# Layer trunk on one Trainium2 core: output projection of the mixer with unsplit fp32 weights, and PSUM banks as one region in the planned order

## The chip, the cores and the metric

The kernel runs on 1 core of a Trainium2 chip. The metric is device time in microseconds. Before the change it is 1097.59 us, the median of 3 runs (1096.93 to 1097.9).

## The reference

Input x is 256 tokens by 1024 features in fp32. Two layers follow each other; each adds half of a SwiGLU feed-forward, a mixer of two head groups, and half of a second feed-forward. A last RMSNorm gives the output. What matters here, from the reference:

```python
for l in range(DEPTH):                                   # DEPTH = 2
    x = x + 0.5 * swiglu(rms_norm(x, ffn1_norm[l]), ...) # 1024 -> 2816 -> 1024
    h = rms_norm(x, mix_norm[l])
    proj = h @ w_in[l]
    y_rwkv = rwkv7_group(proj[..., :RWKV_IN], ...)       # 512 features, a recurrence over chunks of 64
    y_ret = retnet_group(proj[..., RWKV_IN:])            # 512 features, retention in chunks of 64
    mixed = jnp.concatenate([y_rwkv, y_ret], axis=-1)
    x = x + mixed @ w_out[l]                             # 1024 x 1024
    x = x + 0.5 * swiglu(rms_norm(x, ffn2_norm[l]), ...)
return rms_norm(x, final_norm)
```

## The kernel before, in words

The 256 tokens are two tiles of 128 (t = 0 and 1), and each tile is a stream through the seven stages. `run` lets the two streams take turns, tile 1 two steps behind tile 0, so that both use a piece of weights soon after one another.

All weights lie in HBM as pieces of 128 x 2048 fp32, loaded in halves of 128 x 1024 (512 KB) through SyncE's queue into a ring of three raw buffers (`half`, line 616). ScalarE then rounds a half to fp32r (hi), VectorE subtracts it from the raw half (lo), and hi and lo go into two `wide` buffers of 4 KB per partition. Activations are split in the same way (`split`, line 645). A product of fp32 accuracy is then three fp32r matmuls, ah x wh, ah x wl and al x wh (`mm3`, line 639). A half stays in its two wide buffers until the later tile has used it.

The kernel isn't run in the order in which it is written. Every call is recorded as a node of a plan (`record`, line 231) with a price (`price`, line 291) and with its dependencies (`touch`, line 269, compares partitions and columns of a buffer). `simulate` (line 364) then plays the nodes on five engines, with 43 slots of 2 KB, 22 wide buffers and 8 PSUM banks, and gives each node a start. `schedule` (line 492) does this for several priorities (`GUIDES`, `SERIES`) and keeps the one whose modelled end is earliest. `emit` (line 512) issues all nodes in the order of their modelled starts; the tile framework under it then puts the semaphores, and does so by the order of emission. What `behind` and `in_turn` add are edges of the plan alone.

The steps around the change: `norm_T` (line 680) transposes a tile's x by TensorE, four blocks of 128x128 into one bank twice, and ScalarE and VectorE read each block into `parts` (hi and lo). `shifted` (line 766) and `ret_core` (line 1217) also fill a bank by several products and read it block by block. `rms`, `rwkv_key`, `ret_core` and `chain_out` raise a few numbers to -1/2 on GpSimd (`pow`, with operands named base in the trace). `inverse` (line 975) sends blocks through DRAM by SyncE's queue (d, mx, misc).

In the mixer (`mix`, line 1266) a string says the order of the steps of a tile: projections m, k, r, q, e, g, v, the retention R, the merge J, the chain a, b, c, and then W and w, the two halves of the output projection (retention heads and RWKV heads). W uses the pair rh, rl that `ret_out` (line 1252) makes; w uses mh, ml of `chain_end` (line 1163). Per tile and layer, W and w are 16 products of a 128x128 block with 512 columns, each three matmuls. Both tiles use the same wide buffers, so a half of w_out is loaded and split once per layer.

Of the kernel before, what the change touches and what calls it, by code (L numbers as in the profile page):

```python
# [12 lines left out]
F32 = mybir.dt.float32  # L13
F32R = mybir.dt.float32r
BF16 = mybir.dt.bfloat16
AF = mybir.ActivationFunctionType
ALU = mybir.AluOpType
# [5 lines left out]
P = 128  # L23
# [5 lines left out]
RW = 512  # L29
HD = 64  # L30
NRAW = 3
XG = (0, 8, 16)
XCUT = (2, 1)
WARM = 1
# [33 lines left out]
    return ap.unsqueeze(2).to_broadcast(shape)  # L68


PLACES = {"slot": (43, 2048), "wide": (22, 4096), "bank": (8, 2048)}
GUIDES = (5, 7, 10, 14, 20, 30)
SERIES = 3
TURN = -1.0
ENGINES = {"tensor": 0, "vector": 1, "scalar": 2, "gpsimd": 3, "sync": 4}

# [106 lines left out]
class Plan:  # L183
# [84 lines left out]

    def touch(self, op, v, write):
        b = v.buf  # L270
        m = v.bits()
        if not b.users or b.users[-1] is not op.node:
            b.users.append(op.node)
        for o, lo, hi, om in b.writes:
            if lo < v.hi and v.lo < hi and om & m:
                self.wait(op, o)
        if b.space == "bank" and op.node.eng == 0 and getattr(b, "tail", None) is not None:
            self.wait(op, b.tail)
        if write:
            for o, lo, hi, om in b.reads:  # L280
                if lo < v.hi and v.lo < hi and om & m:
                    self.wait(op, o)
            for l in (b.writes, b.reads):
                l[:] = [e for e in l if e[0].node is op.node or not (v.lo <= e[1] and e[2] <= v.hi and not e[3] & ~m)]
            b.writes.append((op, v.lo, v.hi, m))
            if b.space == "bank" and op.node.eng == 0:
                b.tail = op
        else:
            b.reads.append((op, v.lo, v.hi, m))

    def price(self, op):
        out, call, eng = op.args[0], op.call, op.eng
        if call == "dma_start":
            v = next(v for v in (op.outs + op.ins))
            n = (v.hi - v.lo) * v.cols[0].size * 4 if v.cols is not None else 65536
            op.cost, op.late, op.n = 60.0, 0.0, n
            op.form = "dma"
            return
        n = int(np.prod(out.shape[1:]))
        small = n < 32  # L300
        op.form = None
        if eng == "tensor":
            l = op.args[1] if call == "transpose" else op.kw["lhsT"]
            rows, cols = l.shape[0], int(np.prod(l.shape[1:]))
            if call == "matmul" and op.kw["rhs"].dt in (F32R, BF16):
                op.cost = 227.0 if n == 512 else 120.0
                op.late = (398 + n) / 2.4
                op.form = (128, 128)
            else:
                rows = 128 if rows > 64 else 64 if rows > 32 else 32  # L310
                cols = 128 if cols > 64 else 64 if cols > 32 else 32
                op.form = (rows, cols)
                op.cost = {(128, 128): 110.0, (64, 128): 55.0, (128, 64): 30.0, (64, 64): 29.0}.get(op.form, 13.0)
                if call == "matmul":
                    op.cost *= 2
                if n == 512:
                    op.cost = 860.0
                op.late = (398 + 2 * n) / 2.4
            op.late += 60
            return  # L320
        srcs = [v for v in op.ins]
        psum = any(v.buf.space == "bank" for v in srcs)
        col = any(v is not op.args[1] and isinstance(v, View) and int(np.prod(v.shape[1:])) == 1 and n > 8 for v in srcs)
        if eng == "scalar":
            op.cost = (193 + 0.742 * n if psum else 198 + 0.833 * n) + (75 if col else 0)
            f = op.args[2]
            op.form = {AF.Silu: "s", AF.Exp: "t"}.get(f)
        elif eng == "vector":
            if call == "tensor_tensor_scan":
                op.cost = 1224.0  # L330
            elif call in ("tensor_scalar", "tensor_copy", "memset") and not psum:
                op.cost = 150 + 0.52 * n
            elif call == "tensor_reduce":
                op.cost = 151 + 1.04 * int(np.prod(op.args[1].shape[1:]))
            elif len(out.shape) > 3 and out.shape[0] == 64:
                op.cost = 150 + 1.77 * n
            else:
                op.cost = 151 + 1.04 * n + (63 if col else 0)
        else:
            op.cost = 1100.0 if call == "memset" else 1000.0  # L340
        op.cost += 20
        op.late = op.cost + 55

# [20 lines left out]
    def simulate(self, prio):  # L364
# [14 lines left out]
        fabric = 0.0  # L379
        self.low = low = {}  # L380
        done, end, t = 0, 0.0, 0.0
# [7 lines left out]
        while done < total:  # L389
# [3 lines left out]
            t = heapq.heappop(events)  # L393
# [5 lines left out]
            for e in range(5):  # L399
# [49 lines left out]
                if form == "dma":  # L449
                    size = n.ops[0].n  # L450
                    begin = max(t, fabric)
                    fabric = begin + size / 330.0
                    land = fabric + (1700.0 if size > 70000 else 2100.0)
                    shift = land - t
                done += 1
                fin = t + dur
# [93 lines left out]
class Trunk:  # L550
    def __init__(self, plan, x, w, vecs, lora, fgain, consts, out):
# [13 lines left out]
        nc.scalar.dma_start(self.c[:, C_ID:C_ID + P], consts[:, C_ID:C_ID + P])  # L565
        self.load_x(0)
        self.raw = base[:, NBASE + 2 * D:].rearrange("p (n i) -> p n i", n=NRAW)
        self.nraw = 0
        self.consts_d = consts
        self.scan = self.c[:, C_SCAN:C_SCAN + 256].bitcast(BF16)  # L570
        nc.vector.memset(self.scan, 1.0)
# [44 lines left out]
    def half(self, i, h):  # L616

        if (i, h) not in self.wq:
# [7 lines left out]
            kind = sum(i % PIECES >= b for b in (33, 33 + FIRST, 46, 50)) % 4  # L626
            hi = self.A.get([P, 1024], "whi", F32R, kind)
            lo = self.A.get([P, 1024], "wlo", F32R, kind)
            nc.scalar.activation(hi, raw, AF.Copy)
            nc.vector.tensor_tensor(lo, raw, hi.bitcast(F32), op=ALU.subtract)  # L630
            self.wq[i, h] = (hi, lo)
        return self.wq[i, h]

    def weights(self, i, col, width):
        h, c = divmod(col, 1024)
        hi, lo = self.half(i, h)
        return hi[:, c:c + width], lo[:, c:c + width]

    def mm3(self, ps, ah, al, wh, wl, start, stop):
        nc = self.nc  # L640
# [522 lines left out]
    def chain_end(self, t, yf, rv):  # L1163
# [8 lines left out]
            nc.tensor.transpose(tr[:, p, :], yn[:, 2 * p:2 * p + 2].rearrange("q h d -> q (h d)"), self.ident)  # L1172
        TT(g, tr, g, op=ALU.mult)
        TT(g, g, bo, op=ALU.add)
        mh = A.get(full, "mh", F32R)
        ml = A.get(full, "ml", F32R)
        self.split(mh, ml, g)
        self.mixw[t] = (mh, ml)

    def ret_qk(self, t, ps):  # L1180
        nc, A = self.nc, self.A
# [70 lines left out]
    def ret_out(self, t, o_ps, rr, sq):  # L1252
# [5 lines left out]
        tr = self.A.bank(full, F32, name="tr")  # L1258
        for j in range(RH):
            nc.tensor.transpose(tr[:, j, :], sq[:, j, :], self.ident)  # L1260
        mh = A.get(full, "rh", F32R)
        ml = A.get(full, "rl", F32R)
        self.split(mh, ml, tr)
        self.mixr[t] = (mh, ml)

    def mix(self, t, base):
        nc, A = self.nc, self.A
        if t == 0:
# [3 lines left out]
            for i in range(2):  # L1272
# [6 lines left out]
            nc.vector.tensor_tensor(self.rkb, self.c[:, C_ONES:C_ONES + P].unsqueeze(1).to_broadcast([P, 4, P]),  # L1279
                                    self.vb(V_RK), op=ALU.mult)  # L1280
        self.norm_T(t, V_MIX)
        for step in PLAN[t]:
            if step in PROJ:
                blk, then = PROJ[step]
# [14 lines left out]
                self.ret_core(t)  # L1299
            else:  # L1300
                half = "Ww".index(step)
                mh, ml = (self.mixr, self.mixw)[half][t]
                for n in range(2):
                    ps = self.A.bank([P, 512], F32, name="gu")
                    for k in range(4):
                        wh, wl = self.weights(base + 13 + 2 * half + n, 512 * k, 512)
                        self.mm3(ps, mh[:, k, :], ml[:, k, :], wh, wl, k == 0, k == 3)
                        if k == 1:
                            yield
                    s = slice(512 * n, 512 * n + 512)  # L1310
# [157 lines left out]
```

## Time and profile before

| | |
|---|---|
| median of 3 runs | 1097.59 us |
| profiled execution, its own time | 1101.27 us |
| its span from first to last instruction | 1099.4 us |
| mean granted TensorE clock | 0.993 of full speed |
| busy: TensorE, weight loads, VectorE, ScalarE, GpSimd | 1062.5, 853.3, 661.4, 599.1, 38.1 us |
| moved by DMA | 181.57 MB, 165 GB/s in the mean |

How to read it: PE is TensorE's matmuls, PEld its weight loads, which overlap with them, DVE VectorE, ACT ScalarE, POOL GpSimd, SP SyncE. Matmuls are pipelined: each lasts longer than the time until the next can start, so busy time holds more than work. The trace names an instruction by tiles, out<-in: gu and acc are PSUM banks of projections and of the down projections, tr of transpositions and small products, wide the split weights, parts the split activations, base a large buffer that holds constants, x, the small columns and the raw ring. All records bear line 544, that of the emission, so tiles tell them apart. Every stop of an engine is put down to the semaphore that came last.

### The profile page before, as it was taken

To read this page: it belongs to the slowest core of one execution; us is meant where nothing else is said; L and a number is where in the kernel's file an instruction comes from. 1 tells how busy PE (TensorE), PEld (TensorE's weight loads), DVE (VectorE), ACT (ScalarE), POOL (GpSimd) and SP (SyncE) were. 2 spreads that over 40 slices of the span, in tenths; PEclk is the share of its full clock that TensorE was granted. 3 is DMA by queue.
4 is the path that set the end of the run, shared out by engine and by line. 5 is a ranking of instruction groups with operands and counts; after the bars stand their busy time and mean duration, and the time that the engine had idled before them with its cause. 6 is when DMAs were issued, how large, how long until landed. Compare 5 with 4: busy or idle time off the path is not lost.

```text
span 1099.4 us, 16122 instructions
## 1 busy us (share of the span) xinstructions
PE 1062.5 (97%) x6253; PEld 853.3 (78%) x6253; DVE 661.4 (60%) x1051; ACT 599.1 (54%) x1012; POOL 38.1 (3%) x44
## 2 busy tenths in 40 slices
PE   7999999899999999999999999999999999999997
PEld 5778888687877788778768887888877778877885
DVE  5656545577868755445555654546887786656532
ACT  6554444585768645444454554447767856454431
POOL 0000000011010000000000000000100100000000
PEclk9999999999999999999999999999999999999999
DMA  6656557443324466546545564665263236655541
GB/s 227 227 191 198 188 178 223 163 148 98 101 81 137 153 194 195 187 144 218 175 154 191 179 192 146 205 218 166 83 200 98 69 116 206 205 198 184 180 153 39
DMA packets 63772, 181.57 MB, mean 165 GB/s; under 512 B 18512, under 2 KB 18896, under 8 KB 63696
## 3 DMA queue, kind: packets, MB, share of 16 engines
q1 hardware_dynamic: 63264, 180.42, 50.8%
q8 instruction: 49, 0.80, 0.3%
q14 instruction: 27, 0.22, 0.1%
q10 hardware_dynamic: 432, 0.13, 0.1%
HBM read 178.17 MB, written 2.36 MB: 164 GB/s over the span
## 4 chain that ended last, share of the span: by engine, by line
PE 66%; DMA 15%; DVE 7%; ACT 5%; issue 5%; POOL 1%; ACTq 0%; POOLq 0%; DVEq 0%; SPq 0%
PE gu L544 39%; PE acc L544 19%; DMA base<-in_w 14%; PE tr L544 5%; DVE wide L544 4%; ACT wide L544 4%; PE ch L544 2%; PE pre L544 1%; POOL base L544 1%; ACT parts L544 1%; DMA base<-in_vecs 1%; DMA mx<-d 1%; DVE parts L544 0%; DMA d<-el 0%; ACT junk L544 0%
## 5 line engine op out<-in xcount | busy, mean ns | idle before, releaser
L544 PE MATMUL gu<-wide,parts 128*128 128x512 f32 (+1 forms) x2784 | 702.7, 396 | 8.0 <-ACT wide L544 2.8
L544 PEld LDWEIGHTS gu<-wide,parts 128*128 128x128 f32 x2784 | 508.6, 189 | 119.4 <-ACT wide L544 4.0
L544 ACT ACTIVATE wide<-base 128x1024 fp32r<-128x1024 f32 x332 | 349.9, 1059 | 333.9 <-DMA base<-in_w 214.3
L544 DVE TENSOR_TENSOR wide<-base,wide 128x1024 fp32r<-128x1024 f32 x332 | 401.2, 1221 | 203.2 <-ACT wide L544 145.7
L544 PE MATMUL acc<-wide,ht 128*128 128x512 f32 x1056 | 279.8, 396 | 0.7 <-ACT wide L544 0.6
L544 PEld LDWEIGHTS acc<-wide,ht 128*128 128x128 f32 x1056 | 196.9, 189 | 44.5 <-DVE wide L544 2.2
L544 DVE TENSOR_TENSOR ht<-tr,ht 128x256 fp32r<-128x256 f32 x88 | 37.0, 420 | 90.6 <-ACT ht L544 90.5
L544 POOL TENSOR_TENSOR base<-base 128x1 f32<-128x1 f32 (+2 forms) x26 | 33.2, 1277 | 977.3 <-DVE base L544 977.3
L544 DVE SCALAR_TENSOR_TENSOR hh<-gu,base,hh 128x256 f32<-128x256 f32 x88 | 42.1, 480 | 25.1 <-ACT hh L544 24.9
L544 ACT ACTIVATE hh<-gu,base 128x256 f32<-128x256 f32 x88 | 40.7, 464 | 28.3 <-PE gu L544 28.1
L544 DVE SCALAR_TENSOR_TENSOR parts<-tr,base,parts 128x128 fp32r<-128x128 f32 x96 | 30.6, 347 | 31.2 <-ACT parts L544 20.1
L544 ACT ACTIVATE parts<-tr,base 128x128 fp32r<-128x128 f32 x96 | 31.8, 365 | 31.7 <-PE tr L544 22.0
L544 PE MATMUL tr<-base,hh 128*128 128x128 f32 x176 | 43.3, 272 | 0.3 <-DVE ht L544 0.3
L544 ACT ACTIVATE ht<-tr 128x256 fp32r<-128x256 f32 x88 | 32.6, 371 | 15.7 <-PE tr L544 15.6
L544 PEld LDWEIGHTS tr<-base,hh 128*128 128x128 f32 x176 | 24.7, 141 | 7.9 <-DVE ht L544 0.8
L544 PE MATMUL tr<-base 128*128 128x128 f32 x96 | 23.2, 302 | 7.3 <-ACT parts L544 3.4
L544 ACT ACTIVATE junk<-base 128x1024 bf16<-128x1024 f32 (+1 forms) x16 | 15.1, 945 | 24.8 <-DVE base L544 24.8
L544 PEld LDWEIGHTS tr<-base 128*128 128x128 f32 x96 | 13.5, 149 | 19.2 <-ACT parts L544 8.1
L544 DVE SCALAR_TENSOR_TENSOR base<-acc,base 128x512 f32<-128x512 f32 x16 | 11.0, 688 | 28.2 <-PE acc L544 28.1
L544 PE MATMUL gu<-wide,rh 128*128 128x512 f32 x64 | 23.6, 439 | 0.4 <-DVE mi L544 0.4
L544 DVE SCALAR_TENSOR_TENSOR shd<-tr,base,shd 128x127 f32<-128x127 f32 x56 | 17.7, 343 | 9.7 <-ACT shd L544 9.6
L544 PE MATMUL gu<-wide,mh 128*128 128x512 f32 x64 | 20.9, 403 | 0.8 <-ACT mh L544 0.8
(149 smaller groups left out, 595.9 us busy)
## 6 DMA issues: line engine op xcount, KB each, us to landing
base<-in_w SPq DMA_DIRECT2D x328, 512.0 KB, 4.4
base<-in_w SPq DMA_DIRECT2D x8, 256.0 KB, 5.6
lora<-in_lora SPq DMA_DIRECT2D x4, 256.0 KB, 6.2
d<-el SPq DMA_DIRECT2D x8, 128.0 KB, 2.5
out<-ot SPq DMA_DIRECT2D x4, 256.0 KB, 2.0
base<-in_consts SPq DMA_DIRECT2D x1, 805.0 KB, 7.3
base<-in_x SPq DMA_DIRECT2D x2, 256.0 KB, 3.1
base<-in_x SPq DMA_DIRECT2D x1, 512.0 KB, 6.6
```

The costliest lines, as they stand in the source:

```text
L544: getattr(getattr(nc, op.eng), op.call)(*args, **kw)
```

## The change

The change has three parts. First, the output projection of the mixer multiplies with fp32 weights as they are loaded, one fp32 matmul in place of three fp32r ones. `plain` loads a half of w_out into a ring `whole` of three halves, for each tile anew; the activations `g` and `rm` stay fp32 and aren't split. To make room, slots go from 43 to 41 and wide buffers from 22 to 20. Second, `touch` treats a PSUM bank as one region: partitions and columns don't count, and a reader waits in the plan for every earlier write of the bank by another engine. Third, the plan's prices: GpSimd's pow and memset by size, DMAs at 290 bytes per ns and 2.0 us behind (330 and 1.7 or 2.1 before), eight guides and four rounds in place of six and three. The halves of the first two pieces are split in two steps of 512 columns, as they are loaded.

```diff
-PLACES = {"slot": (43, 2048), "wide": (22, 4096), "bank": (8, 2048)}
-GUIDES = (5, 7, 10, 14, 20, 30)
-SERIES = 3
+PLACES = {"slot": (41, 2048), "wide": (20, 4096), "bank": (8, 2048)}
+GUIDES = (5, 7, 10, 14, 20, 25, 30, 40)
+SERIES = 4
...
     def touch(self, op, v, write):
         b = v.buf
-        m = v.bits()
+        bank = b.space == "bank"
+        m, lo, hi = (1, 0, P) if bank else (v.bits(), v.lo, v.hi)
...
-        for o, lo, hi, om in b.writes:
-            if lo < v.hi and v.lo < hi and om & m:
+        for o, a, z, om in b.writes:
+            if a < hi and lo < z and om & m:
                 self.wait(op, o)
-        if b.space == "bank" and op.node.eng == 0 and getattr(b, "tail", None) is not None:
-            self.wait(op, b.tail)
...
             for l in (b.writes, b.reads):
-                l[:] = [e for e in l if e[0].node is op.node or not (v.lo <= e[1] and e[2] <= v.hi and not e[3] & ~m)]
-            b.writes.append((op, v.lo, v.hi, m))
-            if b.space == "bank" and op.node.eng == 0:
-                b.tail = op
+                l[:] = [e for e in l if e[0].node is op.node or (bank and e[0].node.eng == op.node.eng)
+                        or not (lo <= e[1] and e[2] <= hi and not e[3] & ~m)]
+            b.writes.append((op, lo, hi, m))
...
-            op.cost = 1100.0 if call == "memset" else 1000.0
+            op.cost = 100 + 0.83 * n if call == "memset" else 560 + 195.0 * n
...
-                    fabric = begin + size / 330.0
-                    land = fabric + (1700.0 if size > 70000 else 2100.0)
+                    fabric = begin + size / 290.0
+                    land = fabric + 2000.0
...
+        self.whole = plan.fixed([P, NWHOLE, 1024], F32, "whole").rearrange("p n i -> p n i")
...
-            nc.scalar.activation(hi, raw, AF.Copy)
-            nc.vector.tensor_tensor(lo, raw, hi.bitcast(F32), op=ALU.subtract)
+            for c in range(0, 1024, cut):
+                s = slice(c, c + cut)
+                nc.scalar.activation(hi[:, s], raw[:, s], AF.Copy)
+                nc.vector.tensor_tensor(lo[:, s], raw[:, s], hi[:, s].bitcast(F32), op=ALU.subtract)
...
+    def plain(self, i, h):
+
+        w = self.whole[:, self.nwhole % NWHOLE]
+        self.nwhole += 1
+        self.nc.sync.dma_start(w, self.w_d[i][:, 1024 * h:1024 * h + 1024])
+        self.nc.behind(self.begun)
+        return w
...
-        mh = A.get(full, "mh", F32R)
-        ml = A.get(full, "ml", F32R)
-        self.split(mh, ml, g)
-        self.mixw[t] = (mh, ml)
+        self.mixw[t] = g
...
-        mh = A.get(full, "rh", F32R)
-        ml = A.get(full, "rl", F32R)
-        self.split(mh, ml, tr)
-        self.mixr[t] = (mh, ml)
+        self.mixr[t] = A.get(full, "rm")
+        nc.scalar.activation(self.mixr[t], tr, AF.Copy)
...
         self.norm_T(t, V_MIX)
+        if t == 0:
+            self.begun = nc.nodes[-1]
...
-                mh, ml = (self.mixr, self.mixw)[half][t]
+                m = (self.mixr, self.mixw)[half][t]
                 for n in range(2):
                     ps = self.A.bank([P, 512], F32, name="gu")
                     for k in range(4):
-                        wh, wl = self.weights(base + 13 + 2 * half + n, 512 * k, 512)
-                        self.mm3(ps, mh[:, k, :], ml[:, k, :], wh, wl, k == 0, k == 3)
+                        if k % 2 == 0:
+                            w = self.plain(base + 13 + 2 * half + n, k // 2)
+                        nc.tensor.matmul(ps, lhsT=m[:, k, :], rhs=w[:, 512 * (k % 2):512 * (k % 2) + 512], start=k == 0, stop=k == 3)
```

## Rows read from the trace of the kernel before

**Rows 1.** Page, section 1: engine, busy us, share of the span.

```profile
PE 1062.5 (97%) x6253; PEld 853.3 (78%) x6253; DVE 661.4 (60%) x1051; ACT 599.1 (54%) x1012; POOL 38.1 (3%) x44
```

**Rows 2.** Groups by shape, TensorE: operation, out<-in, count | busy us, mean ns | idle before.

```profile
L544 PE MATMUL gu<-wide,parts 128*128 128x512 f32 x2688 | 692.1, 400 | 8.0 <-ACT wide L544 2.8 <-DVE wide L544 1.8 <-DVE hh L544 1.5
...
L544 PE MATMUL gu<-wide,rh 128*128 128x512 f32 x64 | 23.6, 439 | 0.4 <-DVE mi L544 0.4
...
L544 PE MATMUL gu<-wide,mh 128*128 128x512 f32 x64 | 20.9, 403 | 0.8 <-ACT mh L544 0.8
L544 PE MATMUL gu<-wide,parts 128*128 128x256 f32 x96 | 17.0, 282 | 0.0
...
L544 PE MATMUL tr<-bn,rkb 128*128 128x128 f32 x32 | 4.4, 277 | 1.2 <-DVE lw L544 1.2
```

**Rows 3.** Chain that ended last, in time: start us, us, what and count.

```profile
1050.76 37.88 PE acc L544 x167
```

**Rows 4.** Waits of TensorE's matmuls: us in total, times, longest us.

```profile
PE tr L544 <- ACT parts L544: 3.4, 5, 2.1
...
PE tr L544 <- DVE parts L544: 2.7, 5, 1.7
PE tr L544 <- ACT sq L544: 2.5, 2, 1.8
PE tr L544 <- ACT rsq L544: 2.3, 5, 0.5
...
PE tr L544 <- DVE lw L544: 1.2, 1, 1.2
PE gu L544 <- ACT mh L544: 0.8, 1, 0.8
PE tr L544 <- DVE rsq L544: 0.8, 1, 0.8
```

**Rows 5.** Waits of TensorE's weight loads: us in total, times, longest us.

```profile
PEld tr L544 <- ACT parts L544: 8.1, 14, 2.6
...
PEld tr L544 <- DVE parts L544: 5.8, 8, 2.1
...
PEld tr L544 <- ACT rsq L544: 4.1, 8, 0.6
```

**Rows 6.** Timeline of TensorE at three stops: start us, us, instructions, [idle before <-releaser].

```profile
197.74 0.33 PE L544 MATMUL tr<-base 128*128 128x128 f32 x1 [1.70 <-DVE parts L544]
197.82 0.48 PE L544 MATMUL acc<-wide,ht 128*128 128x512 f32 x1
...
308.86 0.49 PE L544 MATMUL tr<-rv,sc 128*128 128x128 f32 x2 [0.46 <-ACT rsq L544]
...
565.97 0.33 PE L544 MATMUL tr<-base 128*128 128x128 f32 x1 [2.13 <-ACT parts L544]
```

**Rows 7.** Windows of 10 us: each engine's busy us, PEclk (granted clock), DMA share, GB/s.

```profile
200.00:210.00 10.00, 9.97 (x48) 7.67 (x48) 4.89 (x10) 3.96 (x7) 1.46 (x1) 0.88 0.48 156
260.00:270.00 10.00, 8.23 (x49) 6.63 (x48) 6.17 (x12) 5.12 (x15) 3.33 (x3) 0.83 0.15 52
```

**Rows 8.** Timeline, 305.3 to 306.6 us, TensorE: start us, us, instructions.

```profile
305.69 0.83 PE L544 MATMUL tr<-bn,rkb 128*128 128x128 f32 x6
```

**Rows 9.** Groups by shape, VectorE: the splits of weights.

```profile
L544 DVE TENSOR_TENSOR wide<-base,wide 128x1024 fp32r<-128x1024 f32 x332 | 401.2, 1221 | 203.2 <-ACT wide L544 145.7 <-PE acc L544 26.0 <-PE gu L544 26.0
```

**Rows 10.** Page, section 6: DMA issues, count, KB each, median us to landing.

```profile
base<-in_w SPq DMA_DIRECT2D x328, 512.0 KB, 4.4
```

**Rows 11.** Timeline of TensorE at the start.

```profile
9.80 0.79 PE L544 MATMUL gu<-wide,parts 128*128 128x512 f32 x1 [2.76 <-ACT wide L544]
```

**Rows 12.** Groups by shape, GpSimd.

```profile
L544 POOL TENSOR_TENSOR base<-base 128x8 f32<-128x8 f32 x8 | 16.8, 2095 | 110.4 <-DVE base L544 110.4
...
L544 POOL MEMSET tt<- 128x512 f32 x4 | 2.1, 529 | 25.3 <-ACT rsq L544 8.3 <-PE pre L544 7.9 <-PE tr L544 6.1
```

**Rows 13.** Waits of all engines: who waited for whom, us in total, times, longest.

```profile
ACT parts L544 <- DVE parts L544: 9.5, 18, 1.2
```

More of the change, by code (lines that the diff above doesn't have):

```diff
@@ L31 @@
 NRAW = 3
+NWHOLE = 3
 XG = (0, 8, 16)
@@ L270, in touch @@
         b = v.buf
-        m = v.bits()
+        bank = b.space == "bank"
+        m, lo, hi = (1, 0, P) if bank else (v.bits(), v.lo, v.hi)
         if not b.users or b.users[-1] is not op.node:
             b.users.append(op.node)
-        for o, lo, hi, om in b.writes:
-            if lo < v.hi and v.lo < hi and om & m:
+        for o, a, z, om in b.writes:
+            if a < hi and lo < z and om & m:
                 self.wait(op, o)
-        if b.space == "bank" and op.node.eng == 0 and getattr(b, "tail", None) is not None:
-            self.wait(op, b.tail)
         if write:
-            for o, lo, hi, om in b.reads:
-                if lo < v.hi and v.lo < hi and om & m:
+            for o, a, z, om in b.reads:
+                if a < hi and lo < z and om & m:
                     self.wait(op, o)
             for l in (b.writes, b.reads):
-                l[:] = [e for e in l if e[0].node is op.node or not (v.lo <= e[1] and e[2] <= v.hi and not e[3] & ~m)]
-            b.writes.append((op, v.lo, v.hi, m))
-            if b.space == "bank" and op.node.eng == 0:
-                b.tail = op
+                l[:] = [e for e in l if e[0].node is op.node or (bank and e[0].node.eng == op.node.eng)
+                        or not (lo <= e[1] and e[2] <= hi and not e[3] & ~m)]
+            b.writes.append((op, lo, hi, m))
         else:
-            b.reads.append((op, v.lo, v.hi, m))
+            b.reads.append((op, lo, hi, m))
     def price(self, op):
@@ L567, in __init__ @@
         self.raw = base[:, NBASE + 2 * D:].rearrange("p (n i) -> p n i", n=NRAW)
-        self.nraw = 0
+        self.nraw = self.nwhole = 0
+        self.whole = plan.fixed([P, NWHOLE, 1024], F32, "whole").rearrange("p n i -> p n i")
         self.consts_d = consts
```

## The prediction

> **What bounds the kernel now.** The page's first section comes first: TensorE is busy for 1062.5 us of a span of 1099.4 [rows 1], so it sets the time, and an edit counts by what it adds to or takes from TensorE's own queue. The second view, the groups of its instructions by shape, says what that queue holds [rows 2]; the chain's longest unbroken piece gives their pace, 37.88 us for 167, so 0.227 us for a 128x512 product of split weights [rows 3]. Busy time overstates here: 3936 such products (2688 of the projections and gate/up, 1056 of the down projections by the code, 8 passes x 11 x 4 x 3, and 192 of the output projection: 64 each of rh and mh, 32 each of rl and ml [rows 2]) come to 893 us, and the small products don't fill the other 206. So the third view is the waits of TensorE, which say who ended each stop [rows 4, 5], the timeline at two stops [rows 6] and the granted clock [rows 7]. The profiled execution took 1101.27 us, 3.7 above the median of the three timed runs (1097.59). The sum is made against 1101.3, and 3.7 is taken off at the end.
>
> **Part 1: unsplit weights, work on TensorE.** 192 products of rh, rl, mh and ml go, 192 x 0.227 = 43.6 us. In their place stand 64 fp32 products of 512 columns. The trace has none so wide. The nearest is bn x rkb: the code issues 16 of them and the trace has 32 records, so two records make one fp32 product [rows 2]. Six records in a row take 0.83 us from the first's start to the last's end, 0.275 of it the last one, so 0.111 apart for 128 columns [rows 8]. Scaled to 512 columns that is 0.444, or 0.888 a product, the upper bound. If a record took 512 columns at the split product's pace, it would be 2 x 0.227 = 0.454, and the part would gain 14.5 us. Against that: a 128-column fp32 record lasts 277 ns, a 256-column one of split weights 282 [rows 2], so fp32 passes columns at about half the rate, which gives four times 0.213 (512 columns at 2.4 GHz) to 0.227, some 0.85 to 0.91. I take 0.87, near the row: 64 x (0.87 - 0.681) = **+12.1 us**, with ends of +10.8 and +14.6 (and the far end -14.5). The Trainium skill (FP8 and Floating Point Precision, TensorE Precision Notes) says that true fp32 takes four passes through the array, against the three that the split pays. By that rule at 0.227 a pass a product would be 0.908 and the part +14.5. The trace shows two records, and cannot tell passes within one.
>
> **Part 1: work on the other engines.** 16 halves of w_out are no longer split: 16 x 1.22 = 20 us of VectorE [rows 9] and a little less of ScalarE, all in the tails of the two mixers, and VectorE loses the lo parts of eight activations, ScalarE four hi parts. None of it is on the path by itself. What it buys is shorter queues: TensorE waited 0.8 us for mh and 1.2 for lw of VectorE [rows 4]. The wait for mh goes with its cause (-1); for lw and the shorter waits beside it I count another -1 (**-2 us** together, ends 0 and -3). W no longer holds 16 of 22 wide buffers from tile 0's use to tile 1's, which lets the second feed-forward's weights in sooner.
>
> **Part 1: what it adds.** 32 loads in place of 16 (each tile loads its own), 8.4 MB on 181.6. A half feeds two products, 1.74 us; a load lands 4.4 us after issue [rows 10]. With a ring of three, a third comes round in 3 x 1.74 = 5.2 us if TensorE does nothing else, and needs 1.74 + 4.4 = 6.1: 0.9 us of waiting per turn, 0.3 per half, 32 x 0.3 = 10 us at worst, and nothing where other products lie between. I take **+1.5**. These loads wait on SP for a product to free their third, and the loads of the next feed-forward and the DMAs of the inverse (d, mx, misc) stand behind them on the same queue; VectorE waits for those. `behind` only puts them after tile 0's norm in the plan, and is no wait on the chip. Wide buffers go from 11 halves to 10; the nearest row is the wait for a first split at the start, 2.76 us [rows 11], and I add **+1** (0 to +3). Slots lose two, but mh, ml, rh and rl give back more.
>
> **Part 2: a bank is one region.** The planner thinks that a reader of the first quarter of a bank needs only the first transposition, so it puts reads between the writes. On the chip the next write then waits for that read: at 197.74 a transposition stops TensorE for 1.70 us until VectorE's read of the quarter before it is over, and products that need nothing of it stand behind; at 308.86 a head of the retention stops for ScalarE's rsq, which reads the head before it [rows 6]. In norm_T, shifted and ret_core all writes of a bank are recorded before its reads, so with one region no read can be planned between them, and these stops are gone by construction. Their idle time is 3.4 + 2.7 + 2.3 = 8.4 us in 15 stops [rows 4]; the loads waited 18.0 us in 30 stops for the same three [rows 5], but some of that lay under products in flight. A stop also costs up to 0.16 us that counts as busy (a 128x512 product lasts 0.39 and the next could start at 0.227), so 30 x 0.16 = 4.8 at most. I take **-12 us**, ends -8.4 and -18.
>
> **Clock.** After two such stops, and two others, TensorE's clock is granted at 1.2 GHz instead of 2.4: windows of 10 us at 0.95 and 0.88 from 190, 0.83 from 260, 0.83 from 310, 0.88 and 0.95 from 560, six windows of which two stand [rows 7]; together 0.68 x 10 = 6.8 us, 1.7 for each of four falls. Those at 199 and 567 follow stops by parts: **-3.4**.
>
> **Part 3: prices.** A pow of 128x8 took 2.1 us and a memset of 128x512 0.53 [rows 12], where the planner assumed 1.0 and 1.1. It now assumes 2.1 and 0.55. Because of the old price the transposition of sq was queued too early: TensorE stood 2.5 us before it, and 0.8 before the rsq transposition, whose pow has the same fault [rows 4]. I count 60% of 3.3 + 0.5, **-2.3**, and 60% of the clock falls at 264 and 315, **-2.0**. The first four halves are split in pieces of 512: the first product waits 2.76 us for a split of 1024 columns [rows 11], half of which is enough. That is some 1 us, and the loads behind it may take it back: **-0.7** (0 to -1.5). The slower modelled DMA moves loads earlier in the queues, for which no row gives a price, and I take 0. A wider search changes the order everywhere, and old stops reappear elsewhere: **+2** (-3 to +6).
>
> **Sum.** 12.1 - 2 + 1.5 + 1 - 12 - 3.4 - 2.3 - 2.0 - 0.7 + 2 = -5.8. 1101.3 - 5.8 = 1095.5, less 3.7: **1092 us**, 0.5% faster.
>
> **Rivals.**
> *The ring paces the projection (slower).* If in the tails little else is ready while tile 1's chain runs, each half waits for its load: +10 in place of +1.5, and the stops of part 2 give only the idle time of the fourth group (-8.4) [rows 4] with one clock fall (-1.7). 12.1 - 2 + 10 + 1 - 8.4 - 1.7 - 2.3 - 2 - 0.7 + 2 = +8, so **1106**. It decides from the point where less than 4.4 us of other products lie between the freeing of a third and its next use. For it: the tails are where TensorE already stops most. Against it: the norm and the feed-forward of the other tile can now stand between, since the wide buffers are free for its weights. Chance 0.24.
> *The stops move (no change).* TensorE waited because nothing else was ready; only the idle 8.4 and one clock fall of 1.7 come back, and prices give 1.5: about **1098**. Part by part: 12.1 - 2 + 1.5 + 1 - 8.4 - 1.7 - 1.5 - 0.7 = +0.3. For it: the stop of 2.13 us at 565.97 falls where one tile's feed-forward ends and the other's has only begun [rows 6]. Against it: right behind the transposition that stopped at 197.74 stood products of the other tile's down projection. Chance 0.14.
> *The plan now fits (much faster).* With right prices the remaining stops go too: part 2 at -16, all four clock falls, no new stops, VectorE's relief in full: 12.1 - 3 - 16 - 6.8 - 3.8 - 1 + 1 = -17.5, so **1080**. Chance 0.13.
> *The change doesn't do what it says.* The region covers writes against reads. Reads of one bank by two engines also go one after the other: ScalarE waited 9.5 us for VectorE's reads of parts in 18 stops [rows 13], and no plan knows of it. If the stops of TensorE came down to these, part 2 would give under 4 us and no clock fall of its own: 12.1 - 2 + 1.5 + 1 - 4 - 2.3 - 2 - 0.7 = +3.6, about **1101**. The stops shown are writes behind reads [rows 6], and those are ordered anew. Chance 0.05. The Trainium skill (PSUM — Partial Sum Buffer, PSUM bank collisions raise a hardware error) asks for a guard by bank and quadrant between any two engines, reads against reads included. By that rule the 9.5 us stay after the change; the trace agrees that such reads are kept apart.
>
> **How the numbers follow.** The forecast (1086 to 1096) has 0.44. The range takes in most of all but the ends: **1081 to 1107**. A measurement of this kernel can tell some 0.2%, 2.2 us. Faster by more (under 1095.4): the forecast (0.44) and the fitting plan (0.13), with 0.01 from the edges: 0.58. Within: the stops that move, 0.14. Slower: the ring and the change that misses, less that edge: 0.28.
>
> **What would show it.** No waits of TensorE for parts or rsq among its first ones; 128 records of gu<-whole some 0.43 us apart (0.227 would make the time some 26 us lower, 0.5 some 9 higher); 312 splits of 1024 columns and 8 of 512 in place of 332; granted clock 1.00 from 190 to 210 and from 560 to 580; 32 loads of whole, and waits of TensorE for them under 3 us in all. Waits of over 8 us for whole mean the first rival. The prediction is wrong if the stops for parts go and the span does not fall by them less the 12 us.

## The result and the profile after

| | before | after |
|---|---|---|
| median of the runs of this comparison | 1097.26 us | 1079.05 us |
| their spread | 1094.49 to 1097.9 | 1076.82 to 1081.28 |
| ratio, with its 95% interval | | 0.9839 (0.981 to 0.9867) |
| profiled execution, its own time | 1101.27 us | 1077.87 us |
| its span | 1099.4 us | 1076.0 us |
| mean granted TensorE clock | 0.993 | 0.997 |
| TensorE idle (span less busy) | 36.9 us | 18.0 us |

The change takes 1.6% off, some 18 us, where the forecast had 5.8 us and the range ended at 1081. Rows of before are named by their groups, as in the prediction.

The page of after, its first section (engine, busy us, share of the span), two of its costliest groups and two of its DMA issues (count, KB each, median us to landing):

```profile
PE 1058.0 (98%) x6189; PEld 840.8 (78%) x6189; DVE 641.8 (60%) x1031; ACT 580.4 (54%) x996; POOL 34.6 (3%) x44
...
L543 PE MATMUL gu<-whole,rm 128*128 128x512 f32 x64 | 33.7, 639 | 0.0
...
L543 PE MATMUL gu<-whole,g 128*128 128x512 f32 x64 | 30.6, 600 | 0.1
...
base<-in_w SPq DMA_DIRECT2D x312, 512.0 KB, 4.3
whole<-in_w SPq DMA_DIRECT2D x32, 512.0 KB, 4.8
```

Against [rows 1] the span fell by 23.4 us, and 18.9 of it is idle time of TensorE that went. Its busy time fell by 4.5 although its work grew by 11 (below): the clock gives back 5, and for the other 11 no row stands alone. That they are records stretched beside stops, which the prediction priced at 4.8 at most, is not shown. VectorE lost 20 us and ScalarE 19, as costed.

The fp32 products in the timeline of TensorE, after (start us, us, instructions):

```profile
350.34 3.59 PE L543 MATMUL gu<-whole,g 128*128 128x512 f32 x8
...
867.79 3.70 PE L543 MATMUL gu<-whole,g 128*128 128x512 f32 x8
```

Eight records are four products. The last record lasts about 0.60, so the first row puts them (3.59 - 0.60) / 7 = 0.427 us apart and the second 0.443; the undisturbed starts of the trace lie 0.429 apart. That is 0.858 us a product, and 64 x (0.858 - 0.681) = +11.3 us.

Who ended TensorE's matmul waits, after (us in total, times, longest); all shorter ones are left out:

```profile
PE gu L543 <- ACT wide L543: 2.0, 1, 2.0
PE tr L543 <- DMA base<-in_consts: 1.8, 1, 1.8
PE pre L543 <- DVE base L543: 1.6, 1, 1.6
PE pre L543 <- issue: 1.4, 1, 1.4
PE tr L543 <- DVE rsq L543: 0.8, 2, 0.4
PE gu L543 <- ACT gg L543: 0.6, 1, 0.6
```

The first three are the start of the kernel. The waits of transpositions for parts and for ScalarE's rsq and sq, which led [rows 4], are gone, and of VectorE's rsq the 0.8 us stayed. Of the weight loads' waits [rows 5] all three rows are gone, and the waits of weight loads for ScalarE and VectorE add up to 26.2 us in place of 54.5. Those that the trace puts down to nothing grew from 14.2 to 39.9, 13.8 of them around the products of whole.

Windows of 10 us, after (busy us of each engine, then PEclk, DMA share and GB/s):

```profile
200.00:210.00 10.00, 10.00 (x75) 8.65 (x74) 6.84 (x19) 7.48 (x19) 0.25 (x1) 1.00 0.81 275
260.00:270.00 10.00, 10.00 (x68) 8.14 (x69) 7.99 (x11) 8.75 (x15) 0.00 (x0) 1.00 0.69 222
310.00:320.00 10.00, 8.54 (x221) 5.94 (x220) 6.83 (x12) 8.50 (x19) 0.00 (x0) 0.91 0.51 164
...
560.00:570.00 10.00, 10.00 (x48) 8.20 (x47) 5.21 (x7) 4.76 (x8) 0.00 (x0) 1.00 0.50 157
```

Where [rows 7] had 0.88 and 0.83, two windows stand at 1.00, and so does 560 to 570. Of four falls to 1.2 GHz one is left, behind a stop of 1.35 us at 316.7 that the trace puts down to nothing: 5.1 us at 1.7 each.

The weight loads' one wait for the ring, after:

```profile
PEld gu L543 <- DMA whole<-in_w: 0.4, 1, 0.4
```

**What moved that the prediction did not price.** A row of before that it did not read says it. ScalarE's timeline ahead of the two longest stops of [rows 6], before:

```profile
195.72 1.06 ACT L544 ACTIVATE wide<-base 128x1024 fp32r<-128x1024 f32 x1 [1.29 <-DMA base<-in_w]
196.69 0.61 ACT L544 ACTIVATE parts<-tr,base 128x128 fp32r<-128x128 f32 x2
...
564.61 1.06 ACT L544 ACTIVATE wide<-base 128x1024 fp32r<-128x1024 f32 x1 [1.74 <-DMA base<-in_w]
565.57 0.35 ACT L544 ACTIVATE parts<-tr,base 128x128 fp32r<-128x128 f32 x1
```

In front of its read of the bank, ScalarE stood 1.29 and 1.74 us at a split whose half had not landed. The plan prices such a load too short: 512 KB at 330 bytes per ns plus 1.7 us are 3.3 us, where these two took 4.4 and 5.9 from issue to landing, and the median is 4.4 [rows 10]. ScalarE works in the order of the plan, so its read, whose block TensorE had finished, queued behind the split. At the first stop TensorE waited for a read of VectorE's, and this one waited for ScalarE's:

```profile
197.33 0.35 DVE L544 SCALAR_TENSOR_TENSOR parts<-tr,base,parts 128x128 fp32r<-128x128 f32 x1 [1.59 <-ACT parts L544]
```

TensorE's stops bear the name parts. If each split had found its half landed, the reads would have come earlier by these 1.29 and 1.74 us: an estimate from the rows, which leaves some 0.4 us of either stop. ScalarE's waits for loads in the view of all engines' waits, before and after:

```profile
ACT wide L544 <- DMA base<-in_w: 214.3, 162, 4.9
```

```profile
ACT wide L543 <- DMA base<-in_w: 124.4, 112, 2.9
```

### The profile page after: what moved, and what is told of

Read it like the earlier page. It is cut to its first block, busy times and chain, and to the rows that moved or that the text cites. A ratio compares the mean times of both kernels' runs of the same rounds, so it can differ in the third digit from the quotient of the medians.

```text
span 1076.0 us, 15951 instructions
## 1 busy us (share of the span) xinstructions
PE 1058.0 (98%) x6189; PEld 840.8 (78%) x6189; DVE 641.8 (60%) x1031; ACT 580.4 (54%) x996; POOL 34.6 (3%) x44
## 2 busy tenths in 40 slices
DMA packets 66075, 189.95 MB, mean 177 GB/s; under 512 B 18768, under 2 KB 19152, under 8 KB 66000
## 4 chain that ended last, share of the span: by engine, by line
PE 89%; DMA 4%; DVE 3%; ACT 2%; issue 1%; POOL 1%; POOLq 0%; ACTq 0%; SPq 0%; DVEq 0%
PE gu L543 58%; PE acc L543 22%; PE tr L543 6%; DMA base<-in_w 2%; PE pre L543 1%; PE ch L543 1%; DVE wide L543 1%; ACT wide L543 1%; POOL base L543 1%; DMA mx<-d 1%; ACT parts L543 0%; DVE base L543 0%; DMA base<-in_consts 0%; DMA misc<-d 0%; DMA d<-el 0%
## 5 line engine op out<-in xcount | busy, mean ns | idle before, releaser
L543 PE MATMUL gu<-wide,parts 128*128 128x512 f32 (+1 forms) x2784 | 688.9, 396 | 3.1 <-ACT wide L543 2.0
L543 DVE TENSOR_TENSOR wide<-base,wide 128x1024 fp32r<-128x1024 f32 (+1 forms) x320 | 382.5, 1208 | 214.4 <-ACT wide L543 129.6
L543 ACT ACTIVATE wide<-base 128x1024 fp32r<-128x1024 f32 (+1 forms) x320 | 332.2, 1047 | 276.6 <-DMA base<-in_w 124.4
L543 PE MATMUL acc<-wide,ht 128*128 128x512 f32 x1056 | 256.7, 391 | 0.0
L543 POOL TENSOR_TENSOR base<-base 128x1 f32<-128x1 f32 (+2 forms) x26 | 29.8, 1145 | 978.9 <-DVE base L543 978.9
L543 PE MATMUL tr<-base,hh 128*128 128x128 f32 x176 | 39.8, 271 | 0.1
L543 PE MATMUL gu<-whole,rm 128*128 128x512 f32 x64 | 33.7, 639 | 0.0
L543 PE MATMUL gu<-whole,g 128*128 128x512 f32 x64 | 30.6, 600 | 0.1
L543 DVE TENSOR_TENSOR base<-gu,base 128x512 f32<-128x512 f32 x16 | 11.0, 690 | 22.7 <-PE gu L543 22.6
L543 ACT ACTIVATE shd<-tr,base 128x128 f32<-128x128 f32 x56 | 17.8, 363 | 10.5 <-PE tr L543 4.4
L543 DVE SCALAR_TENSOR_TENSOR base<-acc,base 128x512 f32<-128x512 f32 x16 | 11.0, 687 | 17.7 <-PE acc L543 17.5
```

The lines of the kernel that those rows point to most:

```text
L543: getattr(getattr(nc, op.eng), op.call)(*args, **kw)
```

## The experiments

Four parts can be made alone: R, the bank as one region; P, the prices with the halved first splits; S, the wider search; W, the unsplit weights with the smaller places. An order is known by its value of GUIDES and by its round, the pass of SERIES that refined it. The first theory (the prediction's, A) was that R carries the gain. Of the rivals that the expectations letter, B says that W is the gain, by relief of the splitting engines; C that each time is a draw among orders; D that the order that before keeps, of value 7 in GUIDES, happens to be a bad one. Later ones say that the old rules stop on the chip whatever the value, and that R and P each cure it (E); that P gains because ScalarE stands in order behind loads that the plan thinks landed (F); or that P gains by GpSimd's prices (G).

Differences in us are (1 - ratio) x 1097.3, each ratio against before of the same comparison. Every search keeps one order; before keeps one of value 7, after one of 40.

**Each part alone, and the change without it.** First R alone:

```diff
 def touch(self, op, v, write):
-        m = v.bits()
+        bank = b.space == "bank"
+        m, lo, hi = (1, 0, P) if bank else (v.bits(), v.lo, v.hi)
...
```

> The kernel before with the bank region in touch alone; weights split, prices and search as before. Theory A (the stops behind reads of the same bank were the gain, and were sized too low: 16 us of stops and two or more clock falls of 1.7): 1097 - 18 = about 1079, no wait of TensorE for parts or rsq. Theory B (the unsplit weights are the gain, by freeing wide buffers, ScalarE and VectorE): about 1092. Theory C (any new order moves the time by several us, and parts don't add up): anywhere from 1085 to 1100, with new stops of another kind.

1075.57 us, ratio 0.9808 (0.9787 to 0.9829): 21 us, more than the whole change. It keeps an order of value 30, third round. Its first waits of TensorE's matmuls:

```profile
PE tr L542 <- DVE hh L542: 4.1, 3, 2.5
PE gu L542 <- ACT wide L542: 2.9, 1, 2.9
...
PE tr L542 <- DVE rsq L542: 1.6, 2, 1.1
```

No transposition waits for parts: the stops of [rows 6] go by R alone, as the prediction had it. W alone:

```diff
-PLACES = {"slot": (43, 2048), "wide": (22, 4096), "bank": (8, 2048)}
+PLACES = {"slot": (41, 2048), "wide": (20, 4096), "bank": (8, 2048)}
...
-        self.mixw[t] = (mh, ml)
+        self.mixw[t] = g
...
-                        self.mm3(ps, mh[:, k, :], ml[:, k, :], wh, wl, k == 0, k == 3)
+                        nc.tensor.matmul(ps, lhsT=m[:, k, :], rhs=w[:, 512 * (k % 2):512 * (k % 2) + 512], start=k == 0, stop=k == 3)
...
```

> The kernel before with the unsplit weights of the output projection alone (ring of three, 41 slots, 20 wide buffers). Theory A: TensorE pays 64 x (0.86 - 0.681) = 11.5 us and little comes back, so 1105 to 1109, with the waits for parts and rsq still there. Theory B: 1090 or below, as the tails get shorter. Theory C: 1100 to 1115.

1099.98 us, 1.0034 (1.002 to 1.0049). B falls: W alone gains nothing. A's 1105 to 1109 was missed too. The change without R, that is with the old `touch`:

```diff
-        m, lo, hi = (1, 0, P) if bank else (v.bits(), v.lo, v.hi)
+        m = v.bits()
...
```

> The changed kernel with the old touch (partitions and columns of a bank counted). Theory A: the stops return, 1079 + 18 = about 1097. Theory B: about 1085. Theory C: 1082 to 1100.

1079.17 us, 0.9845 (0.9824 to 0.9867), the same as the change with R and outside what A and B expected, though its matmuls still wait for a bank's reads:

```profile
PE tr L545 <- ACT rsq L545: 1.7, 5, 0.6
...
PE tr L545 <- ACT parts L545: 1.5, 3, 0.8
```

So R is not the only thing that pays. Without it too, the stops that it forbids have shrunk from [rows 4]. The change without W:

```diff
-PLACES = {"slot": (41, 2048), "wide": (20, 4096), "bank": (8, 2048)}
+PLACES = {"slot": (43, 2048), "wide": (22, 4096), "bank": (8, 2048)}
...
-        self.mixw[t] = g
+        self.mixw[t] = (mh, ml)
...
```

> The changed kernel with split weights in the output projection, as before (22 wide buffers, 43 slots), region, prices and search kept. Theory A: 1079 - 11 = about 1068, faster than both. Theory B: 1088 or more, since the relief of VectorE and of the wide buffers is gone. Theory C: 1070 to 1090.

1074.96 us, 0.9795 (0.9767 to 0.9823): some 5 us below the change. P alone:

```diff
-            op.cost = 1100.0 if call == "memset" else 1000.0
+            op.cost = 100 + 0.83 * n if call == "memset" else 560 + 195.0 * n
...
-                    fabric = begin + size / 330.0
-                    land = fabric + (1700.0 if size > 70000 else 2100.0)
+                    fabric = begin + size / 290.0
+                    land = fabric + 2000.0
...
```

> The kernel before with the new prices alone (GpSimd, DMA, the first halves split in pieces); it keeps a plan of the value 14 in GUIDES. Theory A: 1097 less 4 to 6 for the pow stops and the start, so 1091 to 1093. Theory D: 14 lies between, 1088 to 1095. If the prices themselves are the gain that stands in for the region: 1080.

1073.92 us, 0.9796 (0.9757 to 0.9835), with an order of value 14: 22 us from a few constants and the halved first splits. S alone:

```diff
-GUIDES = (5, 7, 10, 14, 20, 30)
-SERIES = 3
+GUIDES = (5, 7, 10, 14, 20, 25, 30, 40)
+SERIES = 4
```

> The kernel before with the wider search alone (eight values in GUIDES, four rounds); the plan that it keeps comes from the value 30, where the kernel before keeps one of the value 7. Theory A (the region is what removes the stops): 1093 to 1097, the waits for parts and rsq stay near 8 us. Theory D (the plan of the value 7 is what is bad on the chip, and every part of the change that moves the choice to 25 or more gains): 1078 to 1084 without any region.

1086.42 us, 0.9892 (0.9834 to 0.995), in runs from 1078.0 to 1090.51. It runs an order that the old rules make too (value 30, fourth round), so an order by itself can be worth some 10 us: C has something in it, and each part must be read at equal values. In this order no matmul waits for parts either, without R.

**The same value for all rules.** Before with value 30 alone, then R with 7; before and R with 14; P with 7 and with 30.

```diff
-GUIDES = (5, 7, 10, 14, 20, 30)
-SERIES = 3
+GUIDES = (30,)
+SERIES = 2
```

> The kernel before, made to take a plan of the value 30 (GUIDES holds 30 alone, two rounds), nothing else changed. Theory A: 1093 to 1099. Theory D: 1078 to 1085.

```diff
-GUIDES = (5, 7, 10, 14, 20, 30)
+GUIDES = (7,)
```

> The kernel before with the bank region, made to take a plan of the value 7 in GUIDES as the kernel before does. Theory A: 1076 to 1081, as with the region and a free choice. Theory D: 1090 or more, since the value and not the region sets the time.

In the next four the same line holds (14,), (14,), (7,) and (30,), over the old rules, R, P and P.

> The kernel before, made to take a plan of the value 14 in GUIDES; nothing else changed. With 7 it takes 1097 and with 30 it takes 1101. Theory E (the old rules give orders that stop on the chip whatever the value, and the region and the prices each cure that): 1090 to 1105. Theory C (orders are draws that spread over some 25 us under any rules): as likely 1080 as 1100.

> The kernel before with the bank region, value 14. With the region 7 takes 1083 and the free choice, a plan of 30, takes 1076. Theory E: 1074 to 1085, with no wait of TensorE's transpositions for parts or rsq. Theory C: anywhere from 1075 to 1100.

> The kernel before with the new prices, value 7. Theory E: 1072 to 1085, against 1097 for the old prices at the same value. Theory C: anywhere from 1073 to 1100.

> The kernel before with the new prices, value 30. Theory E: 1072 to 1085, against 1101 for the old prices at the same value. Theory C: anywhere from 1073 to 1100.

Median us, and the ratio with its interval; the cells of R with 30 and P with 14 are the two parts alone of above, which keep these values, and before stands for the old rules with 7:

| value | old rules | R | P |
|---|---|---|---|
| 7 | 1097, 1 | 1083.22, 0.9873 (0.984 to 0.9906) | 1079.59, 0.9847 (0.9816 to 0.9878) |
| 14 | 1092.14, 0.9956 (0.993 to 0.9983) | 1086.14, 0.9896 (0.9861 to 0.9932) | 1073.92, 0.9796 (0.9757 to 0.9835) |
| 30 | 1101.06, 1.0036 (1.002 to 1.0051) | 1075.57, 0.9808 (0.9787 to 0.9829) | 1083.03, 0.988 (0.9845 to 0.9914) |

By rows of the table R gives 13.9, 6.6 and 25.0 us, 15 in the mean; P gives 16.8, 17.6 and 17.1. Within a column times differ by 9 to 11 us. Three expectations were missed by 1 to 2 us: the old rules with 30, and R with 7 and 14.

The pairs have equal values, but not all equal rounds: at 30 the old rules run the second round (two were allowed) and R the third, and at 14 the old rules run the third and R the second. S alone is one more order of the old rules with 30, of the fourth round, and it is 15.8 us below the one in the table; against it R with 30 gives 9 us and P with 30 only 1. So the sizes are known to some 10 us each. In the mean the four orders of the old rules on record take 1094 us, R's three 1082 and P's three 1079. All six differences have one sign and these means lie 12 to 15 us apart, so C as the whole explanation falls; value 30 as such is no better than 7 under the old rules, so D falls as it was put, though before's order is some 3 us worse than that mean.

R takes the stops of transpositions for parts away in all its orders. With value 7 they come back in part as stops of the products, which need the parts themselves, and again a late half stands in front of ScalarE's reads (TensorE's wait, then ScalarE ahead of the second of the four):

```profile
PE gu L542 <- ACT parts L542: 5.5, 4, 1.9
```

```profile
370.02 1.06 ACT L542 ACTIVATE wide<-base 128x1024 fp32r<-128x1024 f32 x1 [2.06 <-DMA base<-in_w]
370.98 1.13 ACT L542 ACTIVATE parts<-tr,base 128x128 fp32r<-128x128 f32 x4
```

**Which price.** At value 7 and the old `touch`, the DMA price alone, the GpSimd prices alone, and then the landing of a large load planned 1.0 us earlier than before has it, and later than after has it. The edit for the earliest also plans small transfers 1.4 us earlier (0.7 in place of 2.1):

```diff
-                    land = fabric + (1700.0 if size > 70000 else 2100.0)
+                    land = fabric + 2000.0
```

(and 290 for 330)

> The kernel before with the new DMA price alone (290 bytes per ns and 2.0 us), value 7. Theory F (ScalarE stands in order behind loads that the plan thinks landed, and the reads of banks queue behind it): 1078 to 1084, ScalarE's waits for loads fall from 214 us to 160 or less, and TensorE's waits for parts to 2. Theory G (GpSimd's prices are the gain): 1092 to 1098.

```diff
-            op.cost = 1100.0 if call == "memset" else 1000.0
+            op.cost = 100 + 0.83 * n if call == "memset" else 560 + 195.0 * n
```

> The kernel before with GpSimd's new prices alone, value 7. Theory F: 1091 to 1096, the waits for sq gone, the rest unchanged. Theory G: 1078 to 1084.

```diff
-                    land = fabric + (1700.0 if size > 70000 else 2100.0)
+                    land = fabric + 700.0
```

> The kernel before with a landing time 1.0 us shorter than the old one for large loads (330 bytes per ns and 0.7 us), value 7, nothing else changed. Theory F: worse than before, 1102 or more, ScalarE's waits for loads above 214 us. Theory G or C: no rule, 1085 to 1100.

```diff
-                    fabric = begin + size / 330.0
-                    land = fabric + (1700.0 if size > 70000 else 2100.0)
+                    fabric = begin + size / 290.0
+                    land = fabric + 2700.0
```

> The kernel before with a landing time longer than the new one (290 bytes per ns and 2.7 us, so 4.5 for a half where the trace has 4.4), value 7, nothing else changed. Theory F: as good as the new price or better, 1073 to 1083, ScalarE's waits for loads below those of p2_7. Theory G or C: no rule, 1085 to 1100.

The GpSimd prices alone: 1090.56 us, 0.9946 (0.9926 to 0.9967), 6 us, just below F's range and outside G's; no matmul waits for sq any more. The other three stand in a series with before:

| 512 KB planned to land after | median us | ratio | TensorE idle | of it, matmuls waiting for parts, sq, rsq |
|---|---|---|---|---|
| 2.3 us | 1123.37 | 1.0268 (1.0215 to 1.032) | 54.4 us | 16.1 us |
| 3.3 us (before) | 1097.27 | 1 | 36.9 us | 11.9 us, nearly all in [rows 4] |
| 3.8 us (as after) | 1083.89 | 0.9883 (0.9849 to 0.9917) | 26.4 us | 5.3 us |
| 4.5 us | 1081.2 | 0.9863 (0.9832 to 0.9894) | 26.7 us | 5.5 us |

ScalarE's waits for loads in the same order, of the earliest price, of 3.8 us and of 4.5 (before has 214.3):

```profile
ACT wide L544 <- DMA base<-in_w: 297.2, 196, 6.4
```

```profile
ACT wide L544 <- DMA base<-in_w: 167.6, 138, 4.9
```

```profile
ACT wide L544 <- DMA base<-in_w: 83.1, 63, 4.8
```

TensorE's matmul waits, of the earliest price and of 3.8 us, at the four names that led [rows 4]:

```profile
PE tr L544 <- ACT parts L544: 4.7, 7, 1.3
PE tr L544 <- ACT sq L544: 4.1, 2, 3.8
PE tr L544 <- DVE parts L544: 3.7, 5, 1.9
...
PE tr L544 <- ACT rsq L544: 2.4, 5, 0.6
```

```profile
PE tr L544 <- ACT rsq L544: 1.4, 3, 0.5
...
PE tr L544 <- DVE parts L544: 1.0, 4, 0.4
...
PE tr L544 <- ACT parts L544: 0.7, 2, 0.5
...
PE tr L544 <- ACT sq L544: 0.5, 1, 0.5
```

The kernel's work and the old `touch` are the same in all four, and only the order differs. None of these waits of TensorE is for a load, and yet the waits for bank reads follow the price of a load, by way of ScalarE. The price works in both directions: planned 1 us earlier it costs 26 to 29 us more (medians and ratio), half a us later gives 13 back. Not all of the 26 to 29 is the large loads': in that run VectorE waits 19.3 us for the small transfers of `inverse` (misc and mx), 3.3 before. From 3.8 to 4.5 us ScalarE's waits halve once more and the time hardly moves, as TensorE's own waits don't. The three times came out as F had said; ScalarE's 167.6 us missed the expected 160 and TensorE's waits for parts, 2.6 us in all, the expected 2. Each price is one order, so a draw is not excluded for any one step; against it stands that all four keep the sequence. ScalarE's waits alone don't set the time: they are 195.0 us under the old rules with 30 (1101 us) and 190.0 in R alone (1076 us).

**Both, and a better version.** R and P together at value 7, with split weights; then the same with the landing at 2700 and the old search:

```diff
-        m = v.bits()
+        m, lo, hi = (1, 0, P) if bank else (v.bits(), v.lo, v.hi)
...
-GUIDES = (5, 7, 10, 14, 20, 30)
+GUIDES = (7,)
...
-                    land = fabric + (1700.0 if size > 70000 else 2100.0)
+                    land = fabric + 2000.0
...
```

> The kernel before with region and new prices, split weights, value 7. If the two cure the same stops (ScalarE's late reads make the stop, the region takes the place where it shows): 1074 to 1080, little below the 1080 of the prices alone. If they cure different stops, 1097 - 14 - 18 = about 1065.

```diff
-                    land = fabric + 2000.0
+                    land = fabric + 2700.0
```

> The kernel before with region and new prices, split weights, but a landing time of 290 bytes per ns and 2.7 us, and a free choice among six values of GUIDES and three rounds. If the landing time still pays beyond 2.0: 1066 to 1073, the fastest so far. If 2.0 has cured what there was: 1073 to 1080.

The first: 1067.01 us, 0.9722 (0.9697 to 0.9747), 30.5 us, where R and P at this value give 13.9 and 16.8: they add up, and of the 5.5 us of products waiting for parts 0.4 is left. The second: **1059.01 us** (1058.35 to 1060.38), 0.965 (0.9626 to 0.9674), below both kernels by 38 and 20 us and below what was expected. Its search keeps an order of value 20, so how much of the 8 us between the two is the landing and how much the order isn't known. Its page, and all its matmul waits of over 0.5 us:

```profile
PE 1042.9 (99%) x6253; PEld 854.7 (81%) x6253; DVE 666.6 (63%) x1055; ACT 599.9 (57%) x1016; POOL 35.4 (3%) x44
```

```profile
PE gu L542 <- ACT wide L542: 2.3, 1, 2.3
PE pre L542 <- DVE base L542: 1.6, 1, 1.6
PE tr L542 <- DVE sc L542: 0.6, 1, 0.6
```

It multiplies with split weights, and 13.5 us of TensorE's idle time are left, 7.4 of it behind its last matmul and 4.2 in the waits at the start. W on top of it was not tried.

## Why the prediction was wrong

One way from before to after through measured kernels: R and P at value 7 give -30.5; the new search, which takes value 40 in place of 7, gives (0.9795 - 0.9722) x 1097.3 = +8.0; W gives (0.9839 - 0.9795) x 1097.3 = +4.8. Together -17.7. The prediction's terms for the same three steps were -20.4 (-12, -3.4, -2.3, -2.0 and -0.7), +2 and +12.6. Three misses, then, of 10, 6 and 8 us, and the second hid part of the others.

**The step that failed: "The slower modelled DMA moves loads earlier in the queues, for which no row gives a price, and I take 0".** It is worth some 13 us alone, with one order on either side. A row did point to it: ScalarE stood 214 us for loads, and the timeline ahead of two of the stops that the prediction itself quotes shows a bank's read queued behind one. The prediction doesn't speak of that idle time; ScalarE has 500 us to spare in all. What the price moves is the splits, which go later in ScalarE's order: from the earliest price to the latest 196, 162, 138 and 63 of the 332 splits waited for their half. Whether loads are also issued earlier was not read. The bounds that a cost with no row ought to have had were those of the stops for ScalarE and VectorE, and the range was too high for want of them.

**GpSimd's prices**: -4.3 predicted with their clock (of the 3.8 us of stops that it takes 60% of, 0.5 has no row), -6 measured, with one order on either side. Right in kind. The four first halves cut in two changed little at the start: the first product waits 1.95 us for its split, not 2.76 [rows 11], -0.8 for -0.7, but it starts at 9.66 us in place of 9.80, since TensorE waits 1.8 us for the constants in place of 1.2.

**A bank as one region**: -15.4 with two clock falls; 15 in the mean of three pairs, from 7 to 25, and 12 by the means of all orders. The stops of transpositions and their mechanism were right; that their time would come back whole was not, as at value 7 ScalarE's late reads stop the products for 5.5 us instead. The rival by which the change misses, since reads wait for reads, is refuted, although those waits did stay: in the change ScalarE waited 13.0 us in 31 stops for VectorE's reads of parts, after 9.5 in 18 [rows 13]. The Trainium skill (PSUM — Partial Sum Buffer, PSUM bank collisions raise a hardware error) wants reads of a bank by two engines kept apart too; the trace agrees, and they do not reach TensorE.

**W on TensorE**: +12.1 predicted, +11.3 measured, with 128 records 0.43 apart as said. The Trainium skill (FP8 and Floating Point Precision, TensorE Precision Notes) counts four passes; at 0.227 a pass the part would be +14.5, and the measured 0.858 is four times 0.2145, so four passes fit if a pass takes that; the trace shows two records a product and no passes.

**W's relief**: -2, +1.5 and +1 predicted, so +0.5. TensorE's idle time with and without W, in three pairs of one value and one round each: 18.0 against 24.3 (after and after without W), 19.3 against 25.5 (the change without R, and P with 30), 35.0 against 42.3 (W alone, and the old rules with 30). So -6 to -7 in each, and by the ratios W costs +4.8, -3.8 and -0.2 us: about nothing, where +12.6 was forecast. Which of the two does it, 20 us less of splitting on VectorE or the wide buffers that W no longer holds, was not taken apart. The ring is no matter in the change (0.4 us), and in W alone matmuls waited 3.8 us for it; the rival that was given 0.24 is refuted.

**The search**: +2 with an end of -3 to +6; the pair says +8, the same search under the old rules -12. It is a draw, and its ends were too near one another: two orders of one value under the same old rules lie 15.8 us apart.

**Clock**: three falls gone, 5.1 us; two of them were forecast with R, and 60% of the other two with P.

The rival that the plan now fits (1080, with a chance of 0.13) is what came, for a part of its reason and partly by luck: the remaining stops do go with right prices. Its sum left the load price at nothing as well, took the whole +12.1 of W, and counted no new stops where the search cost 8.

What stays open: how much of the search's +8 belongs to the value and how much to the round; the sizes of R and P to better than some 10 us and W's to better than some 5, since each pair is two orders.

## What to carry to other kernels

In a planned order, an engine with time to spare still carries the path when its next instruction waits for a load and a short read stands behind it; so read that engine's waits for loads, and price a load at the landing that the trace shows (4.4 us here; planned at 3.8 and at 4.5 the times were within 3 us of each other). Let the plan treat a resource as the framework guards it, here a PSUM bank as one. And compare rules of a planner at several equal priorities and rounds, for one order against another, of one value and the same rules, is worth up to 15 us here by itself.

## What the runs showed of the hardware that was not expected

An fp32 product of 512 columns is two records 0.429 us apart, each lasting 600 to 639 ns in the mean, so 0.858 against 0.681 for the three of split weights: the split is the faster on TensorE by a fifth, and yet W as a whole cost about nothing. Moving 8.4 MB more (189.95 for 181.57) raised the mean from 165 to 177 GB/s, and the median landing of a 512 KB half that is split did not grow with it: 4.3 us, 4.4 before. The 32 halves of whole took 4.8.
